# Joined norm and logarithm sums, and another opening of a three-block transformer kernel

## The chip, the cores and the metric

The kernel runs as one program on one core of a Trainium2 chip. A core has TensorE (PE in the rows: matmuls; PEld are its weight loads, which run beside them), VectorE (DVE), ScalarE (ACT), GpSimd (POOL) and SyncE (SP). Each engine works through its own instructions in a fixed order, and semaphores make one wait for another. Data comes from HBM by DMA: 16 DMA engines, fed by queues that SyncE, ScalarE or GpSimd start transfers on. The metric is the device time of one execution in microseconds (us), lower is better.

## What is computed

256 tokens of width 1024 go through a first block (four mixers, a feed-forward net, a gated per-layer input) and through two layers of a second block: dilated attention, a mixture of 16 experts, stick-breaking attention, a mixture of 16 experts. The parts that the change touches:

```python
def rmsnorm(x, g):
    x32 = x.astype(jnp.float32)
    y = x32 * lax.rsqrt(jnp.mean(x32 * x32, axis=-1, keepdims=True) + EPS)
    return (y * g.astype(jnp.float32)).astype(x.dtype)
...
def rope_tables(positions):
    inv = 1.0 / (ROPE_THETA ** (jnp.arange(0, QK_ROPE, 2, dtype=jnp.float32) / QK_ROPE))
    ang = positions.astype(jnp.float32)[..., None] * inv
    return jnp.cos(ang), jnp.sin(ang)
...
def layer_norm(x, g, b):
    xf = x.astype(jnp.float32)
    mu = xf.mean(-1, keepdims=True)
    var = jnp.square(xf - mu).mean(-1, keepdims=True)
    return ((xf - mu) * lax.rsqrt(var + LN_EPS) * g + b).astype(x.dtype)
...
def mixer_stick_breaking(x, w_in, w_out):
...
    z = jnp.clip(jnp.einsum('bhnqd,bhnkd->bhnqk', qb, kb).astype(jnp.float32), -SB_CLIP, SB_CLIP)
    sp = jnp.where(strict, jnp.log1p(jnp.exp(z)), 0.0)
    r_in = jnp.einsum('bhnqj,js->bhnqs', sp, suffix)
    att = jnp.where(strict, jnp.exp(z - r_in), 0.0)
```

`r_in` is a sum over the later keys of a row, here a matmul with a triangle of ones. There are 16 heads of width 64.

## The kernel before

Activations lie feature by feature: `x` is 128 partitions x 8 blocks x 256 tokens. Weights come in pieces of 128x2048, as two tiles of 128x1024 (512 KB each), from a list that `sequence` and `later_pieces` write out. For accuracy a weight piece is split (`wsplit`): ScalarE copies it to `whi` in the format F32R, VectorE subtracts to get `wlo`. Activations are split alike, into `x.hi` and `x.lo`. A projection (`proj`, by `mm3`) is then three F32R products for each weight block: whi with x.hi, whi with x.lo, wlo with x.hi. An f32 matmul, used where operands aren't split, shows as two records in the trace.

`piece` keeps one piece ahead: it starts the load and split of the next before the present is used. Loads go out on SyncE's queue in the order of the program and wait for a free `raw` buffer; a `raw` buffer is freed by the subtraction on VectorE, and a `whi`/`wlo` buffer by TensorE's last product with it.

The order on each engine is that of a scheduler that works from the program's order; `behind(...)` holds an instruction back behind another.

- Opening (`first`): SyncE loads `vecs` (gains and small vectors), the first weight tile of `w_a`, x in four parts of 256 KB between the next weight tiles (`part`, L725), constants and the positions in four small transfers (`rope_angles`, L617). GpSimd loads `rb`, the router's bias. While these land, 22 matmuls on ones run (`warm`, L258). `split_gain` makes gain times x, high on ScalarE and low on VectorE (tiles `gate`). `rstd` squares x on ScalarE, adds the squares on VectorE, sums over partitions by f32 matmuls with `ones` (`sc<-half,ones` or `acc<-half,ones`), takes the root on ScalarE and the reciprocal on VectorE. With `halve` it adds the two blocks of each tile first, so two matmuls instead of four. `rope_angles` makes the angles for cosine, then for sine, each with nine or more small VectorE operations.
- Later norms: in `first_tail` (`late`, the feed-forward stage and the one behind it) and in `dilated`, `rstd` is called without `halve`: four matmuls each.
- Second attention (`stick`): queries and keys of the first four heads are projected together (`begin`, `proj_beside`, two 128-blocks at a time, because the normed x arrives block by block), then per group of four heads ("quad"): `scores` of two heads, the value projection, `scores` of the other two, and beside the next group's projections `sums` and `outputs`. `scores` makes the logits `sbz` and their logarithm terms `sbl` (128x384: two row blocks of one head, the first with 128 keys, the second with 256) by absolute value, exponential and logarithm on ScalarE and mask on VectorE; `sums` multiplies `sbl` with the triangle (`k["suffix"]`, 384 columns) and with `ones` (128 columns) in f32.
- Norm over tokens (`token_norm`), at the end of each expert stage: x lies token by token (128 tokens x 1024, two halves `t`); VectorE adds the last experts' sum with a running total (L1820), ScalarE squares. Then for each half: mean, mean square, root, reciprocal, and x times 1/sigma minus mean/sigma, the first 512 columns on ScalarE and the others on VectorE. In the last layer (`along`) gain and offset follow as two passes of VectorE each (L239 `x<-x,s`), and each piece of 512 columns goes to `out`.

## Time and profile before

| what | us |
| --- | --- |
| median of 3 runs | 1289.57 (1289.53 to 1291.12) |
| the profiled execution | 1292.46 |
| its span | 1290.7 |
| TensorE busy in it | 1258.6 |
| VectorE, ScalarE busy | 731.3, 610.2 |
| moved by DMA | 268.28 MB |

The span runs from the first to the last instruction of the profiled execution, which itself is 2.9 us above the median. Busy times of engines overlap. TensorE's own time is counted from modelled ends, so a busy TensorE isn't always at its peak; its granted clock (PEclk) is given as a share of 2.4 GHz, and 0.50 is 1.2 GHz. In time the stages are: the first block's mixers 0 to 306 us (the opening to 36), the feed-forward net 306 to 517, the per-layer input 517 to 541, the first attention 541 to 838, its experts 838 to 984, a norm to 994, the second attention to 1122, routing to 1130, its experts to 1274, the last norm to the end.

### The profile page before, as it was taken

To read this page: it belongs to the slowest core of one execution; us is meant where nothing else is said; L and a number is where in the kernel's file an instruction comes from. 1 tells how busy PE (TensorE), PEld (TensorE's weight loads), DVE (VectorE), ACT (ScalarE), POOL (GpSimd) and SP (SyncE) were. 2 spreads that over 40 slices of the span, in tenths; PEclk is the share of its full clock that TensorE was granted. 3 is DMA by queue.
4 is the path that set the end of the run, shared out by engine and by line. 5 is a ranking of instruction groups with operands and counts; after the bars stand their busy time and mean duration, and the time that the engine had idled before them with its cause. 6 is when DMAs were issued, how large, how long until landed. Compare 5 with 4: busy or idle time off the path is not lost.

```text
span 1290.7 us, 22672 instructions
## 1 busy us (share of the span) xinstructions
PE 1258.6 (98%) x9159; PEld 1043.3 (81%) x9159; DVE 731.3 (57%) x1416; ACT 610.2 (47%) x951; POOL 24.8 (2%) x48
## 2 busy tenths in 40 slices
PE   9999999999999999999999999999998999999995
PEld 7987899999999999999999999855334999754332
DVE  7877667558665545876464646263215677454214
ACT  6674666446544544755454545232115666242112
POOL 0000000000000000000000000002000000002000
PEclk9999999999999999999999999999999999999998
DMA  7452346657486555566464645599999444557893
GB/s 263 147 183 71 109 137 204 187 178 241 142 300 229 178 186 176 185 190 187 141 194 134 194 134 170 166 318 332 358 395 370 131 131 131 191 196 272 331 397 132
DMA packets 91105, 268.28 MB, mean 208 GB/s; under 512 B 26528, under 2 KB 26672, under 8 KB 90736
## 3 DMA queue, kind: packets, MB, share of 16 engines
q1 hardware_dynamic: 86576, 252.80, 58.5%
q0 software_dynamic: 4416, 13.94, 3.2%
q8 instruction: 74, 1.21, 0.4%
q14 instruction: 39, 0.32, 0.1%
HBM read 267.68 MB, written 6.89 MB: 213 GB/s over the span
## 4 chain that ended last, share of the span: by engine, by line
PE 86%; DVE 5%; DMA 4%; ACT 3%; issue 1%; SPq 0%; ACTq 0%; DVEq 0%
PE ps L250 54%; PE acc L250 14%; PE y L250 6%; PE sc L250 4%; PE o L250 2%; PE sd L250 1%; PE o L258 1%; ACT whi L236 1%; DVE wlo L239 1%; PE sc L1265 1%; DMA raw<-e_d 1%; PE tr L250 1%; DMA s<-rows 1%; DMA wlo<-e_gu 1%; DMA raw<-e_gu 1%
## 5 line engine op out<-in xcount | busy, mean ns | idle before, releaser
L250 PE MATMUL ps<-s,whi 128*128 128x256 f32 x2656 | 495.0, 286 | 5.3 <-DVE s L239 2.5
L239 DVE TENSOR_TENSOR wlo<-raw,whi 128x1024 fp32r<-128x1024 f32 x276 | 333.8, 1218 | 258.5 <-ACT whi L236 258.0
L236 ACT ACTIVATE whi<-raw 128x1024 fp32r<-128x1024 f32 x276 | 287.1, 1054 | 307.1 <-PE ps L250 222.9
L250 PEld LDWEIGHTS ps<-s,whi 128*128 128x128 f32 x2656 | 414.9, 190 | 12.3 <-DVE s L239 4.0
L250 PE MATMUL ps<-s,wlo 128*128 128x256 f32 x1328 | 378.2, 285 | 1.3 <-DVE wlo L239 1.3
L250 PEld LDWEIGHTS ps<-s,wlo 128*128 128x128 f32 x1328 | 251.0, 189 | 4.6 <-DVE wlo L239 2.6
L250 PE MATMUL acc<-hid,whi 128*128 128x256 f32 x512 | 93.0, 281 | 0.0
L250 PE MATMUL ps<-whi,s 128*128 128x256 f32 x512 | 92.3, 282 | 0.0
L250 PE MATMUL ps<-raw,xg 128*64 128x512 f32 x344 | 86.2, 597 | 0.0
L250 PEld LDWEIGHTS ps<-whi,s 128*128 128x128 f32 x512 | 78.2, 188 | 1.5
L250 PEld LDWEIGHTS acc<-hid,whi 128*128 128x128 f32 x512 | 79.3, 189 | 0.0
L250 PE MATMUL acc<-hid,wlo 128*128 128x256 f32 x256 | 72.3, 283 | 0.0
L250 PE MATMUL ps<-wlo,s 128*128 128x256 f32 x256 | 71.7, 280 | 0.0
L250 PEld LDWEIGHTS ps<-raw,xg 128*64 128x64 f32 x344 | 25.7, 136 | 43.9 <-issue 40.5
L236 ACT ACTIVATE eh<-ps 128x256 f32<-128x256 f32 x16 | 6.2, 385 | 114.9 <-PE ps L250 114.9
L247 DVE SCALAR_TENSOR_TENSOR eh<-ps,gslot,eh 128x256 f32<-128x256 f32 x16 | 7.7, 484 | 85.2 <-ACT eh L236 85.2
L236 ACT ACTIVATE s<-y 128x512 fp32r<-128x512 f32 x36 | 21.0, 597 | 69.2 <-PE y L250 69.2
L239 DVE TENSOR_TENSOR s<-y,s 128x512 fp32r<-128x512 f32 x36 | 24.3, 686 | 50.6 <-ACT s L236 50.4
L250 PEld LDWEIGHTS ps<-wlo,s 128*128 128x128 f32 x256 | 48.1, 188 | 0.0
L250 PE MATMUL acc<-s,whi 128*128 128x256 f32 x256 | 47.7, 286 | 0.3 <-ACT dprobT L236 0.3
L250 PEld LDWEIGHTS acc<-hid,wlo 128*128 128x128 f32 x256 | 47.9, 187 | 0.0
L250 PE MATMUL y<-raw,hs 128*64 128x512 f32 x180 | 46.7, 600 | 0.0
(407 smaller groups left out, 1748.9 us busy)
## 6 DMA issues: line engine op xcount, KB each, us to landing
raw<-e_gu SPq DMA_DIRECT2D x81, 512.0 KB, 7.9
raw<-w_dil SPq DMA_DIRECT2D x72, 512.0 KB, 4.6
raw<-w_ff SPq DMA_DIRECT2D x64, 512.0 KB, 4.7
raw<-e_d SPq DMA_DIRECT2D x43, 512.0 KB, 10.1
raw<-w_g SPq DMA_DIRECT2D x32, 512.0 KB, 4.0
whi<-e_gu SPq DMA_DIRECT2D x31, 512.0 KB, 8.4
raw<-w_a SPq DMA_DIRECT2D x28, 512.0 KB, 4.8
raw<-w_sb SPq DMA_DIRECT2D x24, 512.0 KB, 7.8
```

Source lines behind the costliest of these rows:

```text
L236: return self.nc.scalar.activation(out, in_, func, **k)
L239: return self.nc.vector.tensor_tensor(out, a, b, op=op)
L247: return self.nc.vector.scalar_tensor_tensor(out, a, s, b, op0=op0, op1=op1, **k)
L250: self.last_mm = self.nc.tensor.matmul(out, l, r, start=first, stop=last, skip_group_check=True).ins,
L258: self.nc.tensor.matmul(p, self.ones_b, r, start=True, stop=True, skip_group_check=True)
L1265: nc.tensor.transpose(pt[:, c * 128:(c + 1) * 128], e[:, order[c]], self.k["ident"])
```

## The change

1. Opening. ScalarE starts x's four transfers ahead of its table load. The first weight tile comes as two transfers of 128x512 and is copied and subtracted in halves, with `split_gain` of two blocks behind each half's copy. The norm sum `rstd` is asked for right behind the first split. GpSimd starts the four position transfers (`rope_load`). Both angles are made at once in 128x2x64, by three-operand operations, and placed behind the last `split_gain`.
2. Norm sums. With `halve`, `rstd` now adds the last square into the total before it adds the halves, so one matmul remains of two; the three later norms are called with `halve` too.
3. Second attention. `sbl` is split into `sblh` and `sbll` (F32R), triangle and ones are copied to F32R, and each product becomes two. `begin` takes all products with `x.hi` first, then those with `x.lo`.
4. `token_norm`. The statistics of both halves are made two wide; in the last layer x plus minus-mean times gain is made while the root is taken, then times 1/sigma plus offset in one pass.
5. The last expert's `down` weights are asked for one step earlier (`down_weights`), `later_pieces` is called there, and `nhalf` is 3 in the second attention; no transfer on SyncE changes its place by this.

```diff
...
             raw = self.raw()
-            self.nc.sync.dma_start(raw[:, :k], src[:, c:c + k])
+            cuts = [slice(0, 512), slice(512, 1024)] if beside and not c else [slice(0, k)]
+            for u in cuts:
+                self.nc.sync.dma_start(raw[:, u], src[:, c + u.start:c + u.stop])
             then = beside and beside(c // 256)
             hi = self.W.tile([128, 1024], F32R, name="whi", bufs=self.nparts)
             lo = self.W.tile([128, 1024], F32R, name="wlo", bufs=self.nparts)
-            self.act(hi[:, :k], raw[:, :k], AF.Copy)
-            self.tt(lo[:, :k], raw[:, :k], hi[:, :k], OP.subtract)
+            for i, u in enumerate(cuts):
+                self.act(hi[:, u], raw[:, u], AF.Copy)
+                if then:
+                    then(i, len(cuts))
+                self.tt(lo[:, u], raw[:, u], hi[:, u], OP.subtract)
             his.append(hi)
             los.append(lo)
-            if then:
-                then()
...
-    def proj_beside(self, ws, kt, x, evacs, step):
+    def proj_beside(self, ws, kt, x, evacs, step, second=False):
 
 
         out = [self.ps() for _ in ws]
-        for k0 in range(0, kt, step):
+        for part in (0, 1) if second else ():
+            for k0 in range(0, kt, step):
+                for w, p in zip(ws, out):
+                    for b in range(2):
+                        for k in range(k0, min(k0 + step, kt)):
+                            for i, xp in ((0, x.lo),) if part else ((0, x.hi), (1, x.hi)):
+                                self.mm(p[:, b * S:(b + 1) * S], self.cut(w[i], k * S + b * 128, 128), xp[:, k],
+                                        not part and i == 0 and k == 0 and b == 0, part == 1 and k == kt - 1)
...
         if halve:
-            for t in both:
-                self.tt(t[:, 0], t[:, 0], t[:, 1], OP.add)
+            if len(both) > 1:
+                self.tt(tot, tot, both.pop(), OP.add)
+            self.tt(tot[:, 0], tot[:, 0], tot[:, 1], OP.add)
...
-    def rope_angles(self):
+    def rope_load(self):
         nc, A = self.nc, self.A
         tmp = self.row()
         pi = tmp[:, 192:].bitcast(I32)
         src = self.ap["pos"]
         for c in range(4):
-            nc.sync.dma_start(pi[32 * c:32 * c + 32], bass.AP(tensor=src.tensor, offset=src.offset + 64 * c,
-                                                              ap=[[0, 32], [1, 64]]))
-        ang, kk, t = (tmp[:, 64 * i:64 * i + 64] for i in range(3))
+            nc.gpsimd.dma_start(pi[32 * c:32 * c + 32], bass.AP(tensor=src.tensor, offset=src.offset + 64 * c,
+                                                                ap=[[0, 32], [1, 64]]))
...
-        for i, (q, sh) in enumerate(((0.25, math.pi / 2), (0.0, 0.0))):
-            r = self.trig[:, i]
-            self.ts(kk, ang, 1.0 / (2 * math.pi), OP.mult, q, OP.add)
-            self.ts(kk, kk, 12582912.0, OP.add, 12582912.0, OP.subtract)
-            for c, src in ((-TWO_PI_1, ang), (-TWO_PI_2, r), (-TWO_PI_3, r)):
-                self.ts(t, kk, c, OP.mult)
-                self.tt(r, t, src, OP.add)
-            self.ts(r, r, sh, OP.add, 3.1415925, OP.min)
-            self.ts(r, r, -3.1415925, OP.max)
-            if i:
-                self.ts(r, r, self.v("rope", 1), OP.mult)
+
+        kk = self.A.tile([128, 2, 64], F32, name="kk")
+        r, both = self.trig, ang[:, None, :].to_broadcast([128, 2, 64])
+        for i, q in enumerate((0.25, 0.0)):
+            self.ts(kk[:, i], ang, 1.0 / (2 * math.pi), OP.mult, q, OP.add)
+        self.ts(kk, kk, 12582912.0, OP.add, 12582912.0, OP.subtract)
+        for c, src in ((-TWO_PI_1, both), (-TWO_PI_2, r), (-TWO_PI_3, r)):
+            self.stt(r, kk, c, src, OP.mult, OP.add)
+        for i, sh in enumerate((math.pi / 2, 0.0)):
+            self.ts(r[:, i], r[:, i], sh, OP.add, 3.1415925, OP.min)
+        self.ts(r, r, -3.1415925, OP.max)
+        self.ts(r[:, 1], r[:, 1], self.v("rope", 1), OP.mult)
...
-        self.table("sqrt_and_others")
         self.sequence()
         x = self.x2()
+        for b in (0, 2, 4, 6):
+            self.tc.keep_in_program_order(nc.scalar.dma_start(x[:, b:b + 2], ap["xT"][:, b:b + 2]))
+        self.table("sqrt_and_others")
...
-            for b in (j, j + 2):
-                nc.sync.dma_start(x[:, b:b + 2], ap["xT"][:, b:b + 2])
-            return lambda: self.split_gain(h, x, "g_mix", range(j, j + 4))
+            return lambda i, n: self.split_gain(h, x, "g_mix", range(j + 4 * i // n, j + 4 * (i + 1) // n))
...
-                w = self.piece(beside=None if i else part)
+                if i == 0:
+                    self.make(1, part)
+                    r = self.rstd(x, 8, 1e-6, D, True)
+                w = self.piece()
                 if i == 0:
                     nc.sync.dma_start(self.cst, ap["consts"])
-                    self.rope_angles()
+                    angles = self.rope_load()
                 if i == 0:
                     self.proj_beside([w], 8, h, [lambda j, p: evac(0, p)], 4)
+                    with self.behind(self.last):
+                        self.rope_angles(angles)
...
-                rs.append(self.rstd(x, 8, 1e-6, D))
+                rs.append(self.rstd(x, 8, 1e-6, D, True))
...
+        if self.dense:
+            self.later_pieces()
         at = self.new_split(8)
         tiles = {}
+        suffix, ones = (A.tile([128, 128], F32R, name=n) for n in ("suffix_r", "ones_r"))
+        nc.vector.tensor_copy(suffix, self.k["suffix"])
+        nc.vector.tensor_copy(ones, self.ones)
...
-                             [ev("q", 0, 0.125), ev("k", 0, 1.0)], 2)
+                             [ev("q", 0, 0.125), ev("k", 0, 1.0)], 2, True)
...
-            ls = [A.tile([128, 384], F32, name="sbl", bufs=6) for _ in ps]
+            parts = [[A.tile([128, 384], F32R, name=n, bufs=4) for n in ("sblh", "sbll")] for _ in ps]
+            ls = [A.tile([128, 384], F32, name="sbl", bufs=2) for _ in ps]
...
+                self.act(hi, l, AF.Copy)
+                self.tt(lo, l, hi, OP.subtract)
+            tiles["z", quad, hp] = zs, parts
 
         def sums(quad, hp):
 
-            for z, l in zip(*tiles["z", quad, hp]):
+            for z, parts in zip(*tiles["z", quad, hp]):
                 pr = self.ps("sc")
-                self.mm(pr[:, :384], self.k["suffix"], l, True, False)
-                self.mm(pr[:, 128:256], self.ones, l[:, 256:384], False, True)
+                for i, l in enumerate(parts):
+                    self.mm(pr[:, :384], suffix, l, i == 0, False)
+                    self.mm(pr[:, 128:256], ones, l[:, 256:384], False, i == 1)
                 self.tt(z, z, pr[:, :384], OP.subtract)
...
+        self.tt(nm, sums[:, :, 0], sums[:, :, 1], OP.add)
+        self.ts(nm, nm, -1.0 / D, OP.mult)
+
+        def centre(t):
+            for c in cols:
+                self.stt(xr[:, t, c], xr[:, t, c], nm[:, t:t + 1], along[0][:, c], OP.add, OP.mult)
+        if along:
+            centre(0)
+        self.tt(u, nm, nm, OP.mult)
+        self.tt(rs, sqs[:, :, 0], sqs[:, :, 1], OP.add)
+        self.stt(rs, rs, 1.0 / D, u, OP.mult, OP.subtract)
+        self.act(rs, rs, AF.Sqrt, bias=self.eps[1e-5])
+        if along:
+            centre(1)
+        nc.vector.reciprocal(rs, rs)
+        if not along:
+            self.tt(nmr, nm, rs, OP.mult)
...
+                if along:
+                    self.stt(xr[:, t, c], xr[:, t, c], rs[:, o], along[1][:, c], OP.mult, OP.add)
+                    nc.sync.dma_start(self.out[t * 128:t * 128 + 128, c], xr[:, t, c])
+                elif n:
                     self.ts(xr[:, t, c], xr[:, t, c], rs[:, o], OP.mult, nmr[:, o], OP.add)
                 else:
                     self.act(xr[:, t, c], xr[:, t, c], AF.Identity, scale=rs[:, o], bias=nmr[:, o])
-                if along:
-                    self.tt(xr[:, t, c], xr[:, t, c], along[0][:, c], OP.mult)
-                    self.tt(xr[:, t, c], xr[:, t, c], along[1][:, c], OP.add)
-                    nc.sync.dma_start(self.out[t * 128:t * 128 + 128, c], xr[:, t, c])
```

ScalarE at the start of the program before (`whi<-raw` is the weights' high copy, `gate` the high part of x, `half` the squares for the norm, `x_74` is x):

```order
L480 ACT_TABLE_LOAD
L236 ACTIVATE whi<-raw 128x1024
L236 ACTIVATE gate<-x_74,vecs 128x256 x2
L236 ACTIVATE half<-x_74 128x512
L236 ACTIVATE gate<-x_74,vecs 128x256 x2
L236 ACTIVATE half<-x_74 128x512
L236 ACTIVATE whi<-raw 128x1024
L236 ACTIVATE gate<-x_74,vecs 128x256 x2
```

and after (`x_73` is x):

```order
L738 DMA x_73<-xT 128x512 x4
L495 ACT_TABLE_LOAD
L236 ACTIVATE whi<-raw 128x512
L236 ACTIVATE gate<-x_73,vecs 128x256 x2
L236 ACTIVATE whi<-raw 128x512
L236 ACTIVATE gate<-x_73,vecs 128x256 x2
L236 ACTIVATE whi<-raw 128x1024
L236 ACTIVATE gate<-x_73,vecs 128x256 x2
L236 ACTIVATE half<-x_73 128x512
L236 ACTIVATE gate<-x_73,vecs 128x256 x2
L236 ACTIVATE half<-x_73 128x512 x3
```

The four transfers of x stand in front of the table load, the first high copy is cut in two with two blocks of x behind each half, and three squares stand ahead of the next weight piece.

TensorE at the end of the first two projections of the second attention before (`s_10704` is the normed and split x; where it stands first the product belongs to queries or keys, where the weights stand first to values; `sc<-dq,dk`, the first scores, follow 13 value products):

```order
L250 MATMUL ps<-s_10704,whi 128x256 x2
L250 MATMUL ps<-s_10704,wlo 128x256
L250 MATMUL ps<-whi,s_10704 128x256 x2
L250 MATMUL ps<-wlo,s_10704 128x256
L250 MATMUL ps<-whi,s_10704 128x256 x2
```

and after (`s_10685` is the normed and split x):

```order
L250 MATMUL ps<-s_10685,whi 128x256
L250 MATMUL ps<-s_10685,wlo 128x256
L250 MATMUL ps<-s_10685,whi 128x256 x32
L250 MATMUL ps<-whi,s_10685 128x256 x2
L250 MATMUL ps<-wlo,s_10685 128x256
L250 MATMUL ps<-whi,s_10685 128x256 x2
L250 MATMUL ps<-wlo,s_10685 128x256
L250 MATMUL sc<-dq,dk 128x256 x2
```

The products with the low half, spread among the others before, now stand together in one run of 32 at the end; and 6 products of the value projection, instead of 13, come ahead of the first scores.

VectorE in the last norm before (`tn_m` mean, `tn_r` 1/sigma, `tn_u` its square, `tn_b` the shift, `s` gain and offset):

```order
L247 SCALAR_TENSOR_TENSOR tn_r<-tn_r,tn_u 128x1
L239 TENSOR_TENSOR tn_r<-tn_q 128x1
L247 SCALAR_TENSOR_TENSOR tn_r<-tn_r,tn_u 128x1
L1832 RECIPROCAL tn_r<-tn_r 128x1
L239 TENSOR_TENSOR tn_b<-tn_m,tn_r 128x1
L244 TENSOR_SCALAR x_12315<-x_12315,tn_r,tn_b 128x512
L1832 RECIPROCAL tn_r<-tn_r 128x1
L239 TENSOR_TENSOR x_12315<-x_12315,s_12907 128x512 x4
L239 TENSOR_TENSOR tn_b<-tn_m,tn_r 128x1
L244 TENSOR_SCALAR x_12315<-x_12315,tn_r,tn_b 128x512
L239 TENSOR_TENSOR x_12315<-x_12315,s_12907 128x512 x4
```

and after:

```order
L239 TENSOR_TENSOR tn_m<-tn_s 128x2
L243 TENSOR_SCALAR tn_m<-tn_m 128x2
L247 SCALAR_TENSOR_TENSOR x_12396<-x_12396,tn_m,s_12988 128x512 x2
L239 TENSOR_TENSOR tn_u<-tn_m 128x2
L239 TENSOR_TENSOR tn_r<-tn_q 128x2
L247 SCALAR_TENSOR_TENSOR x_12396<-x_12396,tn_m,s_12988 128x512
L247 SCALAR_TENSOR_TENSOR tn_r<-tn_r,tn_u 128x2
L247 SCALAR_TENSOR_TENSOR x_12396<-x_12396,tn_m,s_12988 128x512
L1877 RECIPROCAL tn_r<-tn_r 128x2
L247 SCALAR_TENSOR_TENSOR x_12396<-x_12396,tn_r,s_12988 128x512 x4
```

Statistics are two wide, the centring passes stand between them, and behind the reciprocal four pieces of one pass remain of eight.

## Rows read from the trace of the kernel before

**Rows 1.** The page, part 4: the chain of waits, share of the span by engine.

```profile
PE 86%; DVE 5%; DMA 4%; ACT 3%; issue 1%; SPq 0%; ACTq 0%; DVEq 0%
```

**Rows 2.** Windows: length, busy us (x) of PE, PEld, DVE, ACT, POOL; PEclk, DMA, GB/s.

```profile
306.00:517.00 211.00, 210.50 (x1728) 207.61 (x1727) 122.21 (x139) 103.05 (x124) 1.25 (x2) 1.00 0.64 208
...
1018.00:1122.00 104.00, 104.00 (x820) 93.25 (x817) 68.53 (x142) 60.78 (x102) 0.00 (x0) 1.00 0.45 143
...
1130.00:1274.00 144.00, 141.96 (x686) 65.30 (x685) 47.51 (x143) 34.40 (x67) 8.27 (x10) 1.00 0.79 289
...
998.00:1001.00 3.00, 3.00 (x15) 3.00 (x16) 2.91 (x8) 2.18 (x3) 0.00 (x0) 0.50 0.04 18
```

**Rows 3.** Chain of waits, the opening (start, length, what).

```profile
1.66 5.85 DMA x<-xT
...
35.00 1.15 DVE wlo L239
```

**Rows 4.** Groups by shape, VectorE, 19 to 36 us (busy, mean ns | idle before).

```profile
L243 DVE TENSOR_SCALAR row<-row 128x64 f32<-128x64 f32 x6 | 1.1, 181 | 0.0
```

**Rows 5.** DMA, 0 to 15 us: GB/s in 40 slices; packets, MB, share by queue.

```profile
GB/s 0 0 0 0 34 213 276 317 339 175 165 71 48 70 18 115 317 388 421 415 410 404 393 393 399 415 459 399 426 404 415 415 397 411 391 398 411 346 415 393
...
q0 software_dynamic: 32, 0.01, 7.5%
```

**Rows 6.** Groups by shape, TensorE, whole span (two records for one f32 matmul).

```profile
L250 PE MATMUL sc<-half,ones 128*128 128x256 f32 x28 | 7.5, 388 | 0.0
...
L250 PE MATMUL acc<-half,ones 128*128 128x256 f32 x16 | 3.9, 379 | 0.0
```

**Rows 7.** Chain of waits at one norm and at the second attention.

```profile
529.31 1.73 PE acc L250 x8
...
997.84 14.35 PE ps L250 x105
...
1018.34 5.95 PE ps L250 x48
1024.29 1.73 PE sc L250 x8
```

**Rows 8.** Timeline, TensorE, the sums of one head (start, length, what).

```profile
1024.13 0.81 PE L250 MATMUL sc<-sbl,consts 128*128 128x384 f32 x2
1024.78 0.38 PE L250 MATMUL sc<-sbl,ones 128*128 128x128 f32 x2
```

**Rows 9.** Timeline, a pair of heads: its last mask, its first sum.

```profile
1039.62 0.49 DVE L239 TENSOR_TENSOR sbl<-sbl,consts 128x128 f32<-128x128 f32 x2
...
1048.44 0.81 PE L250 MATMUL sc<-sbl,consts 128*128 128x384 f32 x2
```

**Rows 10.** Groups, VectorE, 1027 to 1100 us, second attention.

```profile
L239 DVE TENSOR_TENSOR wlo<-raw,whi 128x1024 fp32r<-128x1024 f32 x19 | 23.2, 1223 | 10.2 <-ACT whi L236 10.0
...
L247 DVE SCALAR_TENSOR_TENSOR sbl<-sbz,sbl 128x384 f32<-128x384 f32 x12 | 6.7, 555 | 7.9 <-ACT sbl L236 7.9
```

**Rows 11.** Windows, 24 us of that attention, about one group of four heads.

```profile
1026.00:1050.00 24.00, 24.00 (x192) 21.73 (x191) 17.86 (x38) 16.26 (x28) 0.00 (x0) 1.00 0.42 132
```

**Rows 12.** Timeline, start of the second attention ([idle before <- releaser]).

```profile
996.08 0.39 PE L250 MATMUL ps<-s,whi 128*128 128x256 f32 x1 [1.19 <-DVE s L239]
...
997.84 0.55 PE L250 MATMUL ps<-s,whi 128*128 128x256 f32 x1 [1.14 <-DVE s L239]
...
1001.69 0.42 DVE L239 TENSOR_TENSOR s<-x,s 128x256 fp32r<-128x256 f32 x1
```

**Rows 13.** Chain of waits, the last norm.

```profile
1277.12 0.19 DVE tn_m L239 x2
...
1279.87 1.89 DVE x L239 x3
...
1282.45 2.50 DVE x L239 x4
```

**Rows 14.** Groups by shape, VectorE, three-operand work on 128x512, whole span.

```profile
L247 DVE SCALAR_TENSOR_TENSOR x<-x,s 128x512 f32<-128x512 f32 x8 | 5.1, 686 | 0.9 <-DMA s<-rows 0.9
```

More of the change, by code (lines that the diff above doesn't have):

```diff
@@ L347, in piece, with make @@
     def piece(self, n=1, beside=None):
-        while len(self.made) < n + 1 and self.pieces:
+        self.make(n + 1, beside)
+        now, self.made = self.made[:n], self.made[n:]
+        return now if n > 1 else now[0]
+    def make(self, n, beside=None):
+        while len(self.made) < n and self.pieces:
             src, width = self.pieces.pop(0)
@@ L352, in piece @@
             beside = None
-        now, self.made = self.made[:n], self.made[n:]
-        return now if n > 1 else now[0]
     @staticmethod
@@ L1739, in hidden, with down_weights, down @@
             return hs
-        def down(i, hs):
+        def down_weights(i):
+            return wsp[1] if i == 8 else self.beside([ap["e_d"][layer, 2 * i + s] for s in range(2)], 2048)
+        def down(i, hs, wd=None):
             yparts.append(yparts.pop(0))
             y = yparts[0]
-            wd = wsp[1] if i == 8 else self.beside([ap["e_d"][layer, 2 * i + s] for s in range(2)], 2048)
+            wd = wd or down_weights(i)
             for n in range(2):
```

37 lines of the change are left out of this document (18 added, 19 removed).

## The prediction

> **What bounds the kernel now.** I read the chain of waits by engine first: 86% of the span is TensorE at work or feeding itself [rows 1]. So most stages end when TensorE has worked off its queue, and a matmul taken out is worth its own time there, while work moved among the other engines is worth nothing unless TensorE stands for it. The windows say where that holds: the feed-forward stage keeps TensorE busy 210.50 of 211 us and the second attention 104.00 of 104, with the DMA engines at 0.45 in the latter, while the second expert stage runs its DMA at 0.79 [rows 2]. Three short stretches are bound otherwise, and the change edits each of them. In the opening TensorE waits first for x, which lands 1.66 + 5.85 = 7.5 us after the start, then for VectorE's backlog up to 35.00 + 1.15 = 36.15 us [rows 3]. At the start of the second attention it waits for the low halves of the normed input (1.19 and 1.14 us, [rows 12]) and then runs at a granted clock of 0.50, the 1.2 GHz level, for 3 us [rows 2]. Behind the last matmul, VectorE does the last norm alone: from 1277.12 to 1284.95 us [rows 13].
>
> **Opening.** Two ends meet. For the front: x now goes out on ScalarE's queue instead of between the weight pieces, and the first weights are split in halves. x shares the engines with the weights either way; over 400 GB/s flow from about 6.4 us on, but before that lies a lull down to 18 GB/s [rows 5], so I take no earlier x and 0.4 us for the halves. For the back: VectorE is the bound to 36 us, and 11 of 23 small angle operations go. Six of them are recorded at 181 ns [rows 4]; their records overlap, so I count 0.15 us each, 1.65 us. Against that stand two wider operations, one more 128x512 addition of the sum of squares and the cut subtraction, together about 0.8 us. The reciprocal no longer stands behind the angles, which now come behind the first split. ScalarE squares x before it converts the next weight piece, which holds TensorE up by up to 0.8 us, but the stage ends with VectorE. Net **-0.8 us**, between -1.8 (the removed work whole) and +0.8 (ScalarE's delay whole).
>
> The Trainium skill, "DMA: Bandwidth & Descriptors", section "Issuing engines are not separate DMA queues", says that transfers started by different engines run on the same 16 DMA engines, and that starting them from several saves only issue time. The lull and the plateau of this trace agree with it. By it alone the front gives nothing and the sum below would be 0.4 us smaller.
>
> Positions move to GpSimd's queue behind the router's bias. Off SyncE that frees issue time nobody waits for; what it may cost is rival 1.
>
> **Norm sums.** Three norms (in the feed-forward, behind it, and in the first attention) fold four squares into one before the ones-matmul: 4 f32 matmuls become 1. A group of four takes 1.73 us, 0.43 each [rows 7]. The counts before are 8 and 14 (two records each, [rows 6]); the order shows 2 and 10 after. Of the 10 removed one is in the opening, where TensorE isn't the bound; 9 x 0.43 = **-3.9 us**. VectorE adds a 128x512 and loses none, 0.6 us per norm, in stages where it is busy 122 of 211 us [rows 2]. If a projection's result then waits for the norm for lack of a free PSUM bank, 0.3 us per norm is lost: bounds -3.0 to -4.0.
>
> **Suffix sums of the second attention.** Now each head has one f32 product of 384 columns and one of 128: a head is half of a pair's 1.73 [rows 7], 0.87 us, of which 1024.13 to 1024.78 is the first product, 0.65 [rows 8], and 0.22 the second. After, each is two F32R products, of the high and the low part. F32R at 256 columns goes at 5.95 / 48 = 0.124 us [rows 7]; for 384 I scale it to 0.18. At 128 columns F32R isn't in these rows: from 0.062 (scaled) to 0.22 (what f32 takes at that shape). I take 0.17, halfway from the row of the same format (0.124) to that of the same shape (0.22). 2 x (0.18 + 0.17) = 0.70; 16 heads x 0.17 = **-2.7 us**, between -1.1 and -6.2.
> The parts cost ScalarE a copy and VectorE a subtraction of 128x384, some 0.55 us a head [rows 10], with a new wait: VectorE stands for ScalarE's copy, and behind it in its queue lie the weights' low halves. The cover is large: a pair's last mask starts at 1039.62 and its sum at 1048.44 [rows 9], and two heads' copies and subtractions take 2.2 of those 8 us, 3.5 with two waits of 0.66 (worked out in rival 3). The f32 buffers shrink from six to two, but two heads are in work at a time. So I cost it at nothing; rival 3 is what it costs if the cover is gone.
>
> **Start of the second attention.** The first two projections (96 products) take all products with the high half first (64), then those with the low half (32). Before, four products stand ahead of 997.84 with two waits, 1.19 and 1.14 us [rows 12]; the chain's 105 from there to 1012.19 [rows 7] are the other 92 and 13 of the value projection, so the 96 end at 1012.19 - 13 x 0.124 = 1010.6. After, high products run while the low halves are made; the last of these is done at 1001.69 + 0.42 = 1002.1 [rows 12], and if only the 32 low products are left then, they end at 1002.1 + 32 x 0.124 = 1006.1. With part of the half clock [rows 2] left I take 1007: 3.6 us won. Some comes back, since the high weights are now needed in both passes and their buffers come free later, so the value weights are converted later and the first scores wait for them, by my estimate 0.6 to 1.2 us (a weight piece's high copy and subtraction take turns on both engines; the subtraction takes 1.22 us, [rows 10]). Net **-2.8 us**, between -0.5 (half clock stays and the scores wait 2 us) and -4.0.
>
> **Last norm.** Before, eight two-operand passes stand behind the statistics: 1.89 us for three, 2.50 for four [rows 13]. After, two passes (centre and gain, then scale and offset) of four pieces each, three-operand; these are recorded at 686 ns [rows 14], paced like the others at 2.50 / 4 = 0.62. From 1277.12: mean 0.25, four centred pieces 2.50, beside them two-wide statistics 0.5, reciprocal 0.2, four pieces 2.50: 1283.0 instead of 1284.95, and the wait of about 0.4 us for the root is covered by centring. Outputs now leave 0.62 us apart, about what one 256 KB transfer takes at 400 GB/s, so 0.1 us is lost at the end. **-1.9 us**, between -1.0 and -2.3. The same statistics in the first layer: **-0.2** (0 to -0.5). The earlier asking for the last expert's weights and the smaller buffer count move no transfer: 0.
>
> **Sum.** -0.8 - 3.9 - 2.7 - 2.8 - 1.9 - 0.2 = -12.3 us. The profiled execution took 1292.46 us (span 1290.7), 2.9 over the median of 1289.57; the same steps from the median give **1277.3 us**. All good ends give 1270.3, all bad ones 1284.8.
>
> **Rivals.**
> 1. The four position loads stall the opening. The software queue's 32 packets (8 KB) hold 7.5% of 16 engines for 15 us [rows 5], 1.1 us of all engines, while the rate falls to 18 GB/s. Four more such loads, in front of x and the first weights: up to 4.5 us. For it: the lull is there and nothing else explains it; against: it may be paid once. 1277.3 + 0.8 + 4.5 = **1282.6**. 12%.
> 2. What the second attention gains is lost behind it, because the second expert stage is set by its weights (DMA 0.79, [rows 2]). The 2.7 + 2.8 go: **1282.8**. Against: the weights come as buffers fall free, which TensorE's pace sets, at 0.45 before that stage. 14%.
> 3. Slower: VectorE becomes the bound of the second attention. Per group of four heads (24.3 us, from 1024.13 to 1048.44, [rows 8, 9]) VectorE is busy 17.9 us of 24 [rows 11], idle 6.2. Added are 4 x 0.55 = 2.2 us and 4 waits for the copy, each as long as today's for ScalarE, 7.9 / 12 = 0.66 [rows 10], 2.6 us. If none of the idle time gives way, a group takes 24.3 + 4.8 = 29.1 us; four groups and the lost 2.7 give 1277.3 + 19.2 + 2.7 = **1299.2**. It turns slower than before from 24.3 + 9.6 / 4 = 26.7 us a group. Against: over the 73 us of these rows, three groups, 10.2 of some 18.6 idle us are waits for weights [rows 10] whose buffers TensorE frees, and these shrink. 5%.
> 4. The reordering does not do what it says: the half clock and the buffers eat the whole 2.8, and F32R at 128 columns costs what f32 does (another 1.6): 1277.3 + 4.4 = **1281.7**. 15%; the forecast itself 54%.
>
> **How the numbers follow.** About 0.2%, 2.6 us, is what a measurement of this kernel can tell, so faster means below 1287.0. The forecast and rivals 1, 2 and 4 lie there, unless two of them meet: faster 0.88. Two meeting with the bad ends of other terms: same 0.07; rival 3 past its point: slower 0.05. The range takes in rivals 1, 2 and 4 and half of the good ends: 1272.5 to 1284.5.
>
> **What would show it.** Opening: VectorE's backlog ends near 35.4 instead of 36.15; rival 1 shows as x landing after 9 us. Norms: one ones-matmul where four stood. Sums: the pair's 1.73 us becomes about 1.4. Second attention: no wait for low halves, the first two projections end about 3 us earlier in the stage. End: VectorE's part, from the mean to its last pass, takes 5.9 us instead of 7.8. The prediction is wrong if the expert stages grow by what the stages ahead of them shrink, or if groups of four heads take longer than 24.3 us.

## The result, and the profile after

| | before | after |
| --- | --- | --- |
| median of 4 runs each on one chip, us | 1290.09 (1289.53 to 1291.12) | 1278.74 (1278.42 to 1279.50) |
| ratio after / before | | 0.9912 (95% interval 0.9895 to 0.9929) |
| profiled execution, us | 1292.46 | 1278.75 |
| its span, us | 1290.7 | 1276.8 |

The change takes 11.35 us off (9.2 to 13.5 by the interval); 12.3 were forecast. The two traces differ by 13.9 us, because the profiled execution of before lay above its median and that of after did not. So a stage is judged below by several traces, not by this pair alone. Executions of one kernel differ with the granted clock: of seven executions of before on one chip, three took 1288.96 to 1289.35 us at a mean granted clock of 0.993, and four took 1291.8 to 1292.48 at 0.990 or 0.991.

The page of after, its busy times (part 1) and its chain of waits by engine (part 4):

```profile
PE 1245.2 (98%) x9139; PEld 1037.0 (81%) x9139; DVE 737.0 (58%) x1413; ACT 613.1 (48%) x964; POOL 26.7 (2%) x52
...
PE 83%; DMA 8%; DVE 4%; ACT 3%; issue 1%; SPq 0%; DVEq 0%; ACTq 0%; POOL 0%
```

TensorE is busy for 13.4 us less, 1245.2 instead of 1258.6, and that is nearly the whole difference of the spans; some 3 us of it aren't work taken out but two stretches in which before ran at the lower clock (both below). VectorE and ScalarE are busy for longer. In the chain DMA has 8% instead of 4% [rows 1]. Little of that is the opening, whose DMA link grows from 5.85 to 9.64 us; most are six links of weights from 931.33 to 987.18 us, in the first expert stage and the norm behind it, where before's chain runs over the engines. That stage isn't longer for it: from the first attention's routing to the last expert sums it takes 155.6 us instead of 156.1.

Where the time went, between instructions that both traces name. The third column is the profiled execution of after less that of before (what is not listed makes up the other 0.8 us), the fourth what the experiments leave of it:

| stretch | forecast | the two traces | by the runs below |
| --- | --- | --- | --- |
| opening, to the first matmul on the angles (`sd<-trig,half`) | -0.8 | +0.7 | +0.7, in other traces up to +1.6 |
| 54 to 82 us, where the clock differs | 0 | -1.5 | 0 |
| feed-forward stage, first norm | -1.3 | -1.2 | -1.25 |
| per-layer input to first attention, second and third norm | -2.6 | -1.4 | -1.4 |
| last expert sums to the first scores of the second attention | -3.0 | -3.4 | -3.4 (of it -1.5 by the clock) |
| first scores to the routing | -2.7 | -3.9 | -3.9 (sums -4.65, +0.8 given back) |
| second expert stage | 0 | -1.0 | 0, 148.8 to 150.4 us in all kernels |
| last norm | -1.9 | -1.4 | -1.45 |
| sum | -12.3 | -13.1 | -10.7 |

The sum of the last column and the median agree within 0.7 us. That the sum came out near the forecast is in part luck, since misses of both signs cancel: opening and norm sums brought 2.7 us less than forecast and the last norm 0.4, the second attention 1.6 more, of which 1.5 is a clock that no run ties to the change.

The second line isn't the change. TensorE's granted clock in 54 to 82 us, before and after (windows; columns as in [rows 2]):

```profile
54.00:82.00 28.00, 26.62 (x203) 25.59 (x203) 23.92 (x51) 17.76 (x27) 0.26 (x2) 0.94 0.52 166
```

```profile
54.00:82.00 28.00, 26.62 (x213) 25.10 (x211) 24.76 (x54) 18.79 (x29) 0.26 (x2) 1.00 0.52 169
```

At 0.94 fewer instructions fit into the same 28 us. From the first `sd<-trig,half` to the first `ps<-whi,a4p`, 224 matmul records on, before took 30.2 or 30.3 us in its two traces. Of the kernels below whose TensorE order is after's up to there, five took 30.2 or 30.3 as well (`pos_sync`, `norm3_old`, `begin_old`, `sums_f32`, `lo_twice`), while two (`norm2_old`, `tail_old`) took 28.7, as after itself did in both its traces. So this 1.5 us isn't to be put down to the change.

### The profile page after: what moved, and what is told of

Same layout as the page of the kernel before. It is cut to its first block, busy times and chain, and to the rows that moved or that the text cites. A ratio compares the mean times of both kernels' runs of the same rounds, so it can differ in the third digit from the quotient of the medians.

```text
span 1276.8 us, 22646 instructions
## 1 busy us (share of the span) xinstructions
PE 1245.2 (98%) x9139; PEld 1037.0 (81%) x9139; DVE 737.0 (58%) x1413; ACT 613.1 (48%) x964; POOL 26.7 (2%) x52
## 4 chain that ended last, share of the span: by engine, by line
PE 83%; DMA 8%; DVE 4%; ACT 3%; issue 1%; SPq 0%; DVEq 0%; ACTq 0%; POOL 0%
PE ps L250 54%; PE acc L250 13%; PE y L250 5%; PE sc L250 4%; PE o L250 2%; DMA wlo<-e_gu 2%; DMA raw<-w_sb 1%; PE sd L250 1%; DMA raw<-e_d 1%; PE sc L1289 1%; ACT whi L236 1%; DVE wlo L239 1%; DMA s<-rows 1%; PE tr L250 1%; DMA whi<-e_d 1%
## 5 line engine op out<-in xcount | busy, mean ns | idle before, releaser
L239 DVE TENSOR_TENSOR wlo<-raw,whi 128x1024 fp32r<-128x1024 f32 (+1 forms) x277 | 333.4, 1213 | 243.9 <-ACT whi L236 243.3
L236 ACT ACTIVATE whi<-raw 128x1024 fp32r<-128x1024 f32 (+1 forms) x277 | 286.5, 1049 | 296.9 <-PE ps L250 213.4
L239 DVE TENSOR_TENSOR s<-y,s 128x512 fp32r<-128x512 f32 x36 | 24.2, 685 | 50.6 <-ACT s L236 50.5
```

The lines of the kernel that those rows point to most:

```text
L236: return self.nc.scalar.activation(out, in_, func, **k)
L239: return self.nc.vector.tensor_tensor(out, a, b, op=op)
```

## Experiment: is it the opening, and which part of it?

The forecast was that VectorE's backlog ends near 35.4 us. It ends at 35.69 + 1.15 = 36.84, later than the 36.15 of before [rows 3]. The chain of waits of after in the opening (start us, length, what):

```profile
2.13 9.64 DMA raw<-w_a
...
11.79 1.07 ACT whi L236
...
35.69 1.15 DVE wlo L239
```

The first DMA link is no longer x but the second tile of the first weights, 9.64 us on its way, to 11.77 us. Three kernels take this apart; `before_again` gives before's own spread, with nothing changed.

> The kernel before, unchanged, for a second trace. Theory: the profiled execution of before ran about 2.4 us above its median because of two stretches that belong to that run and not to the kernel, a granted clock of 0.94 in 54 to 82 us (58 products in 8.65 us instead of 7.14) and about 1 us in the second expert stage; the second trace then has a span near 1288.3 us, and the matmuls on a4p that end at 81.1 us end near 79.6. Rival: these stretches are the kernel's, the span is again near 1290.7 and the clock again 0.94 there; then the change gained 13.9 us in the trace and something outside of the span took 2.5 back.

Measured: 1291.04 us, span 1289.3, with the opening at 51.1 us as in the first trace of before. The theory missed on the clock, which was 0.94 in 54 to 82 us again. The span is 1.4 us shorter, 1.1 of it in the two expert stages, where the theory had 1 us in the second.

`old_opening` has the parts of the diff in `wsplit`, `split_gain`, the angles and `first` undone, and nothing else.

> The kernel after with the opening of before (loads, weight halves, order of squares, angles one after the other). Theory: the new opening loses 0.7 us by the time VectorE's backlog ends (36.84 against 36.15 us), so this kernel is 0.7 us faster than the kernel after, about 1278.0, and the product run behind the backlog starts near 36.2 us. Rival (the forecast): the new opening is worth 0.8 us, so this kernel takes about 1279.5.

`pos_sync` moves only the positions back:

```diff
-            nc.gpsimd.dma_start(pi[32 * c:32 * c + 32], bass.AP(tensor=src.tensor, offset=src.offset + 64 * c,
+            nc.sync.dma_start(pi[32 * c:32 * c + 32], bass.AP(tensor=src.tensor, offset=src.offset + 64 * c,
```

> The kernel after with the four position transfers back on SyncE's queue, x still by ScalarE's. If the position transfers on GpSimd's queue hold up the first weights (rival 1 of the prediction), the second weight half lands 1 to 4 us before 9.89 us and the backlog of VectorE ends 1 us or more before 36.84: about 1277.5. If it is x on a queue of its own, with all transfers in flight at once, that makes the weights late, nothing moves before 12 us and the time is that of the kernel after, 1278.7, within 0.5.

`x_sync` moves only x back between the weight tiles on SyncE's queue:

```diff
-        for b in (0, 2, 4, 6):
-            self.tc.keep_in_program_order(nc.scalar.dma_start(x[:, b:b + 2], ap["xT"][:, b:b + 2]))
...
+            for b in (j, j + 2):
+                nc.sync.dma_start(x[:, b:b + 2], ap["xT"][:, b:b + 2])
```

> The kernel after with x back on SyncE's queue between the weight tiles, positions still by GpSimd's. If x on its own queue makes the weights late, the second half lands at about 6 instead of 9.87 us and the second tile near 10 instead of 11.77, the first projection ends about 2 us before 20.1 and VectorE's backlog near 35.5 instead of 36.84: 1277.4. If GpSimd's transfers are the cause, the first half is still late (after 6.2 us) and the backlog ends near 36.8: 1278.7.

Measured, on one chip with before at 1291.8 us (1288.96 to 1292.48):

| kernel | us | ratio to before | backlog ends | `sd<-trig,half` starts |
| --- | --- | --- | --- | --- |
| before | 1291.8 | | 36.15 | 51.1 |
| after | (another chip) | 0.9912 | 36.84 | 51.8 |
| old_opening | 1279.62 | 0.9916 (0.9898 to 0.9934) | 36.19 | 51.1 |
| pos_sync | 1279.17 | 0.9910 (0.9892 to 0.9927) | 36.85 | 51.8 |
| x_sync | 1278.05 | 0.9902 (0.9881 to 0.9923) | 35.16 | 50.1 |

The medians lie within 1.6 us and tell the three apart badly; the traces do it better. The opening of after varies, though: in the nine traces on this page that have x on ScalarE's queue, `sd<-trig,half` starts at 51.8 to 52.7 us, in the middle at 52.3, so +0.7 is the least that it loses against before, which has 51.1 in both its traces. `pos_sync` changes nothing (36.85 against 36.84), so the positions on GpSimd's queue cost nothing that shows beside this spread, far from the 4.5 us of rival 1: it falls. `x_sync` is where the time is. ScalarE's first weight copies in after and in `x_sync` (timeline: start, length, what, in brackets the idle time before it and what ended it):

```profile
6.24 0.63 ACT L236 ACTIVATE whi<-raw 128x512 fp32r<-128x512 f32 x1 [2.32 <-DMA raw<-w_a]
...
9.89 0.63 ACT L236 ACTIVATE whi<-raw 128x512 fp32r<-128x512 f32 x1 [2.22 <-DMA raw<-w_a]
...
11.79 1.06 ACT L236 ACTIVATE whi<-raw 128x1024 fp32r<-128x1024 f32 x1 [0.47 <-DMA raw<-w_a]
```

```profile
5.97 0.63 ACT L236 ACTIVATE whi<-raw 128x512 fp32r<-128x512 f32 x1 [3.94 <-DMA raw<-w_a]
...
7.48 0.63 ACT L236 ACTIVATE whi<-raw 128x512 fp32r<-128x512 f32 x1 [0.87 <-DMA raw<-w_a]
```

With x on a queue of its own, ScalarE gets the second half of the first weights at 9.89 us, 2.4 us later than the 7.48 of `x_sync`, and waits 2.22 us for it. x itself doesn't come late. Its first part with ScalarE's queue (chain of `pos_sync`), and with SyncE's, with the end of the backlog there (chain of `x_sync`):

```profile
0.75 3.94 DMA x<-xT
```

```profile
2.13 6.02 DMA x<-xT
...
34.01 1.15 DVE wlo L239
```

It lands at 4.69 instead of 8.15 us. All 1 MB of x is then in flight beside the weights, though the first two blocks of it are all that the first half needs; on one queue it comes in the order of need. The DMA engines' rate in after (GB/s in 40 slices of 0 to 15 us, as in [rows 5]):

```profile
GB/s 0 0 0 0 34 100 158 251 295 330 354 382 291 205 164 147 160 198 298 344 354 411 384 438 388 403 445 437 396 404 423 396 426 419 430 397 416 405 427 412
```

The rate climbs more slowly, 100 and 158 in the sixth and seventh slice where before had 213 and 276, but the dip behind the first transfers is filled in the main (147 instead of 18). By 6 us, 16 slices, 1.02 MB have come instead of 0.69. So the second queue does bring data earlier, only not the data that the first projection waits for.

What is left of the new opening in `x_sync` is worth -1.0 us against before (50.1 against 51.1), by the end of the backlog too (35.16 against 36.15). That is near the forecast's -0.8 and its 35.4. How much of it the weight halves bring and how much the fewer angle operations, no run separates. The queue for x takes 1.7 us away here.

`after_again` and `x_sync_again` are the same two kernels, on one chip, five executions each, to see whether the version with x on SyncE beats the change.

> The kernel after, unchanged, beside the next one on the same chip. If the stretch from 52 to 80 us at a granted clock of 0.94 or 1.00 comes and goes, its length is 28.7 or 30.2 us whichever the kernel; the opening ends at 51.8 us or a little more as before; total about 1279.

> The kernel after with x back on SyncE's queue, beside the kernel after on the same chip. Theory: its opening ends 1.7 us earlier (50.1 against 51.8), nothing later gives it back, so its median is 1.7 us below that of the kernel after. Rival: a later stage that the weights' transfers bound takes it back, and the two agree within 0.5 us.

Measured beside before at 1290.64 us: after 1279.97 (1279.25 to 1281.63), ratio 0.9922 (0.9908 to 0.9935); with x on SyncE 1277.55 (1276.51 to 1279.69), ratio 0.9900 (0.9886 to 0.9913). The medians differ by 2.4 us and the openings in the traces by 2.5 (52.4 against 49.9); the intervals still touch. In the two traces of `x_sync` the stretch of 54 to 82 us was at the lower clock (30.2 us) and in the two of after at the full one (28.7), so the profiled spans are closer than the medians, 1276.8 each in the first pair. With that said, x on SyncE's queue is the fastest version here, by the opening in both its traces and by the median in both comparisons, the first of them across two chips.

## Experiment: what are the norm sums worth?

All three stand as one matmul (two records) where four stood. After, from the second norm to behind the third (chain of waits; start, length, what):

```profile
526.91 0.43 PE acc L250 x2
527.34 15.75 PE ps L250 x132
543.09 1.19 DVE s L247 x3
544.27 1.18 DVE wlo L239
545.46 0.61 DVE half L239
...
546.20 11.76 PE ps L250 x96
557.96 0.43 PE sc L250 x2
558.39 21.48 PE ps L250 x179
```

Each group takes 0.43 instead of 1.73 us [rows 7], as forecast. The feed-forward stage is indeed 1.25 us shorter, in every kernel that has its norm halved. The other two should give 2.6 together and give 1.4: from the start of the second group to the end of the third, before takes 32.9 us (529.31 to 560.46 + 1.73 = 562.19) and after 31.5 (526.91 to 558.39). In between stands a wait that before doesn't have. After, and before (timeline of TensorE, columns as above):

```profile
546.20 0.47 PE L250 MATMUL ps<-s,whi 128*128 128x256 f32 x2 [1.59 <-DVE half L239]
```

```profile
550.21 0.38 PE L250 MATMUL ps<-s,whi 128*128 128x256 f32 x1 [0.34 <-DVE s L247]
```

1.59 us of waiting instead of 0.34 is the missing 1.2. I first took it that the second norm alone was eaten by a stretch bound by VectorE, and undid one norm at a time.

`norm3_old`:

```diff
-                    r = self.rstd(x, 8, 1e-6, D, True)
+                    r = self.rstd(x, 8, 1e-6, D)
```

> The kernel after, with the third of the later norms (first attention) back at four ones-matmuls. In the trace of after TensorE waits 1.6 us for VectorE's adding of squares (544 to 546 us), which wasn't there before. Theory: that wait eats the 1.3 us of this norm, so from the per-layer products (517.7 before, 515.3 after) to the first attention's value products (588.0, 584.2) this kernel takes 68.9 us as after does, and the time is that of after within 0.3 us. Rival (the forecast): the norm gained its 1.3 us and the stretch takes 70.2 us.

`norm2_old` (`one[0]` is true for the first of these norms and set false behind it):

```diff
-                rs.append(self.rstd(x, 8, 1e-6, D, True))
+                rs.append(self.rstd(x, 8, 1e-6, D, one[0]))
```

> The kernel after with the second of the later norms (behind the feed-forward) back at four ones-matmuls. With the third norm undone, the stretch between the per-layer products and the first attention's value products had grown from 68.9 to 70.1 us, of 70.3 before, so the third norm has its 1.2 us and the second cannot have more than 0.2. Theory: TensorE's saved 1.3 us ends in the 1.59 us wait behind VectorE's drain of a projection (at 546 us), a stretch that VectorE bounds; then this kernel keeps 68.9 within 0.2 us and its wait there shrinks to 0.3. Rival: both norms gained and something else lost; then the stretch takes 70.2.

Measured: 1281.39 and 1280.39 us, one execution each. From the end of the feed-forward stage to the first product behind the third norm's stage, before takes 70.3 us, after 68.9, `norm3_old` 70.2, `norm2_old` 70.1. So each of the two norms is worth 1.2 to 1.3 when the other is there, and my theory that the second was worth nothing falls. Both kernels still wait 1.6 us for `half` at the same product, so the wait belongs to neither of them alone: a kernel with one of them undone is no faster than before in this stretch, because it pays the wait and has one gain to set against it.

What the wait is, the instruction order with its waits shows. The waiting product is the first of a projection: with it 96 products stand in the chain up to the third norm's sum; before, 13 of these ran ahead of its stall, which left 83. TensorE's instructions stand in the same order there in both kernels, but the projection's first product waits for other things. Before, then after:

```
L250 MATMUL ps_6306<-s16_6248,whi_6184 128x256 [waits Activation_49]
```

```
L250 MATMUL ps_6296<-s16_6238,whi_6174 128x256 [waits DVE_49,Activation_49]
```

It now waits for VectorE too, and what VectorE finishes just ahead of 546.20 is `half<-ps,rstd` (L239), the pass that takes the projection just ahead out of PSUM, the memory that matmuls write to. The built programs say why. The waiting projection has PSUM bank 0 in both kernels; the projection just ahead of it has bank 2 in before and bank 0 in after, and there the next one has to wait until VectorE has taken its result out. With only the second or only the third norm as in before, it stays bank 0, as the waits of `norm2_old` and `norm3_old` show. With only the first norm as in before, the program has bank 2 and before's waits again. So it is the first norm's shorter sum that moves the bank, and the 1.2 us would be a price of that norm, nearly all of the 1.25 us that it brings. That kernel was read and not run, so this price is argued, while the wait and its 1.2 us are measured.

## Experiment: the suffix sums

After, the sums of a pair of heads (chain of waits, then the timeline of TensorE):

```profile
1011.64 5.95 PE ps L250 x48
1017.59 1.10 PE sc L250 x8
```

```profile
1017.43 0.34 PE L250 MATMUL sc<-sblh,suffix_r 128*128 128x384 f32 x1
1017.60 0.23 PE L250 MATMUL sc<-sblh,ones_r 128*128 128x128 f32 x1
1017.66 0.39 PE L250 MATMUL sc<-sbll,suffix_r 128*128 128x384 f32 x1
1017.90 0.22 PE L250 MATMUL sc<-sbll,ones_r 128*128 128x128 f32 x1
1017.96 0.39 PE L250 MATMUL sc<-sblh,suffix_r 128*128 128x384 f32 x1
```

From start to start, a product of 384 columns takes 0.17 to 0.24 us and one of 128 columns 0.06. A pair takes 1.10 us instead of 1.73 [rows 7], where 1.40 were forecast.

`sums_f32` has before's f32 products (`sblh`, `sbll` and the F32R copies of triangle and ones are gone), `lo_twice` makes each low part twice, which loads VectorE with as much again:

```diff
-                self.tt(lo, l, hi, OP.subtract)
+                for _ in range(2):
+                    self.tt(lo, l, hi, OP.subtract)
```

> The kernel after with the suffix sums back in f32 (no split of the logarithm terms). After, a pair of heads' sums takes 1.10 us in the chain where before had 1.73. Theory: the eight pairs are all that the sums gained, so from the first attention's router product (825.1) to the second's last (1113.1) this kernel takes 5.0 us more than the 288.0 of after. The forecast had 2.7 us. Rival: the added copies and subtractions cost TensorE waits, then it is less than 5.

> The kernel after with each low part of the logarithm terms subtracted twice: one more VectorE operation of 128x384, 0.55 us, for each of 16 heads. If the 8 us of cover between a pair's last mask and its sum hold, the second attention keeps its length within 0.3 us. If VectorE is near to being its bound (rival 3 of the prediction), each group of four heads grows by up to 2.2 us and the stage by up to 8.8.

Measured: 1283.71 and 1280.24 us, one execution each, before at 1290.97. From the first scores to the routing's last product, after takes 108.40 us, `sums_f32` 113.04, `lo_twice` 108.40. So the split sums are worth 4.65 us, 0.4 less than eight pairs at 0.63 (where that goes stays open), and twice the low part costs nothing: the cover that the forecast counted on holds with room to spare, and rival 3 falls. How VectorE pays for it (groups by shape, 1020 to 1093 us; busy, mean ns, idle before) in `sums_f32`, after and `lo_twice`:

```profile
L239 DVE TENSOR_TENSOR wlo<-raw,whi 128x1024 fp32r<-128x1024 f32 x19 | 23.2, 1223 | 9.9 <-ACT whi L236 9.7
```

```profile
L239 DVE TENSOR_TENSOR wlo<-raw,whi 128x1024 fp32r<-128x1024 f32 x19 | 23.2, 1222 | 3.3 <-ACT whi L236 2.9
...
L239 DVE TENSOR_TENSOR sbll<-sbl,sblh 128x384 fp32r<-128x384 f32 x13 | 7.2, 553 | 0.6 <-ACT sblh L236 0.6
```

```profile
L239 DVE TENSOR_TENSOR wlo<-raw,whi 128x1024 fp32r<-128x1024 f32 x19 | 23.2, 1221 | 0.0
L239 DVE TENSOR_TENSOR sbll<-sbl,sblh 128x384 fp32r<-128x384 f32 x28 | 15.0, 553 | 0.2
```

VectorE's idle time ahead of the weights' low halves shrinks from 9.9 to 3.3 to nothing as the low parts are added, and TensorE's pace stays. The wait for ScalarE's copy, which the forecast bounded by 0.66 us each, is 0.6 us over 13 of them.

## Experiment: the start of the second attention and the norms over tokens

`begin_old` takes the first two projections in before's order (`2, True` becomes `2` in the call); `tail_old` has before's `token_norm`, in both layers.

> The kernel after with the second attention's first two projections in the order of before (high, low and low-weight products together). Forecast: the new order is worth 2.8 us, so the stretch from the norm's statistics to the first scores grows by 2.8 us, with waits for the low halves of about 2.3 us and a stretch at half clock. Rival: the new order gains nothing beyond the two-wide statistics, and the stretch stays within 0.5 us, because weight buffers come free later.

> The kernel after with the norm over tokens of before in both layers. Theory: from the last mean (1264.7) to the end it takes 13.5 us as before instead of 12.1, and from the first layer's running totals (980.7) to the second attention's first scores (1004.74) 25.2 us instead of 24.04, since undoing the order of the first projections gave only 2.2 of the 3.35 us that this stretch gained. Forecast: 14.0 at the end (1.9 us) and 24.2 at the first (0.2 us). Rival for the first: the 1.2 us belong to the earlier asking for the last weights, then it stays at 24.0.

Measured: 1281.13 and 1280.93 us, one execution each. In the table the first column runs from the first read of the last expert sums' total (`tn_s`) to the first scores, the third from the last read of the last norm's totals to the end of the span:

| kernel | to the first scores | first scores to routing | last norm |
| --- | --- | --- | --- |
| before, twice | 27.4, 27.4 | 112.3, 112.2 | 13.6, 13.6 |
| after | 24.0 | 108.4 | 12.2 |
| begin_old | 26.3 | 107.5 | |
| tail_old | 23.6 | | 13.6 |

The order of the products brings 2.3 us up to the scores and gives 0.9 back behind them, 1.4 net. Before's order with everything else of the change is already 1.1 us faster than before, and the chains show how. Before, then `begin_old`:

```profile
997.84 14.35 PE ps L250 x105
```

```profile
995.37 12.84 PE ps L250 x105
1008.21 0.02 issue
1008.23 0.92 PE sc L250 x8
```

The same 105 products behind the same waits take 1.5 us less. Windows of 1 us in before (as in [rows 2]) and in `begin_old`:

```profile
999.00:1000.00 1.00, 1.00 (x7) 1.00 (x6) 0.91 (x3) 1.00 (x2) 0.00 (x0) 0.50 0.01 4
```

```profile
997.00:998.00 1.00, 1.00 (x11) 1.00 (x10) 0.92 (x3) 0.98 (x3) 0.00 (x0) 1.00 0.00 0
```

Before runs these products at a granted clock of 0.50 (1.2 GHz) for some 3 us, in both its traces; `begin_old`, in before's order, at 1.00. In the 3 us ahead (995 to 998 and 992 to 995 us) TensorE was busy 0.78 us in before and 1.01 us in `begin_old`, so it had stood still for most of the time in both. Why the clock falls in one and not in the other, no run here separates, and it stays open; the 1.5 us are therefore not shown to be the change's. In after TensorE is busy 2.69 us of the 4 up to 992, and the products run at 1.00:

```profile
992.45 12.29 PE ps L250 x100
1004.74 0.87 PE sc L250 x8
```

The two-wide statistics don't help at this place: with the old ones (`tail_old`) the scores come 0.4 us earlier in the stretch, where the forecast had -0.2. The shift `tn_b`, which ScalarE's half of the norm waits for, in after and in `tail_old` (timeline of VectorE):

```profile
987.16 0.15 DVE L239 TENSOR_TENSOR tn_b<-tn_m,tn_r 128x2 f32<-128x2 f32 x1
```

```profile
986.25 0.16 DVE L239 TENSOR_TENSOR tn_b<-tn_m,tn_r 128x1 f32<-128x1 f32 x1
```

The total's first read is at 980.70 and 980.80. With one shift for both halves it comes behind one more weight subtraction than the first half's shift had to wait for. So the stretch's -3.4 are -2.3 by the order, -1.5 by the clock and +0.4 by the statistics.

At the end of the program the new `token_norm`, two-wide statistics and single pass together, is worth the whole 1.45 us: 12.2 us with the new form, 13.6 with the old, as in before. The last norm of after (chain; the mean ends at 1264.91):

```profile
1264.74 0.17 DVE tn_m L239
...
1265.19 1.41 DVE x L247 x2
...
1268.06 0.17 DVE tn_r L1877
...
1268.96 2.03 DVE x L247 x3
```

From the mean to the last pass it takes 1270.99 - 1264.74 = 6.25 us, where before took 7.8 [rows 13] and 5.9 were forecast. A centring pass takes 0.70 us (1.41 for two) and not the 0.62 assumed.

## Why the prediction was right, point by point

- **What bounds the kernel** held in the main: TensorE is busy for 13.4 us less and the span fell with it, some 3 us of that by the clock. That the added work of VectorE costs nothing was tried in the second attention (`lo_twice`) and held there.
- **Opening** failed: +0.7 instead of -0.8. The step that failed is "I take no earlier x and 0.4 us for the halves": x's queue was taken as neutral because the engines are shared "either way", and the lull to 18 GB/s was read as agreeing with that. But the lull fills when a second queue is there, x's first part lands 3.5 us earlier, and the weights that are needed ahead of most of x land 2.4 us later. With x back on SyncE the rest of the term held (-1.0).
- **Rival 1** fell: the positions' queue is worth 0.0 us in one pair of traces. Its sign, x landing after 9 us, could not have told it apart: what came late by x's own queue was a weight half, not the first x.
- **Norm sums** had the right price for each matmul (0.43 us) and the right kind of trouble, a projection waiting for a PSUM bank, but not its place and size: "0.3 us per norm", for which the prediction shows no row, was a bound of 0.9 in all, and one wait of 1.2 us more came between the second and the third norm. Measured -2.65 instead of -3.9, outside the bounds of -3.0 to -4.0.
- **Suffix sums** were mis-sized in the term "I take 0.17, halfway": 128 columns in F32R go at 0.06 us, which is the bound scaled by columns from the 256-column row. Measured -4.65 instead of -2.7, inside the bounds.
- **Start of the second attention** came out at -3.4 to the scores, with 0.8 given back behind them: -2.6 against -3.0. The number is near by luck. The scheme (high products first, some of it given back) held in kind, but the order is worth 1.4 net where 2.8 were forecast; the two-wide statistics cost 0.4 instead of bringing 0.2; and 1.5 is the half clock, which is gone in `begin_old` too, without the new order. That the value weights are what gives the time back was not tested.
- **Last norm** -1.45 against -1.9: a wider pass than assumed, 0.08 us each.
- **Rival 2** fell: the second expert stage takes 148.8 to 150.4 us in all kernels, and what the attention gains reaches the end. **Rival 3** fell with `lo_twice`. **Rival 4** fell on F32R at 128 columns, which is cheaper, not dearer; of the reordering's 2.8 us half is there, so on that count it was half right.
- **The bounds**: all good ends add up to 18.8 us, so to 1270.8 and not 1270.3 us; the range doesn't hang on it.

## What to carry to other kernels

A queue of its own brings an early input sooner, and everything on it then competes with what is needed first; so in an opening like this one keep the transfers on one queue in the order of need, and check by the landing time of the first weights. Where an edit shortens TensorE's work, look at the first products behind it for a new wait: here a shorter group shifted the PSUM bank that a later projection gets, and half of the gain of two groups stood there. Cover for added work is best read from the idle time ahead of the engine's own loads, here 9.9 us that shrank to 3.3 with no effect on the pace, and not from its share of busy time.

## What the runs showed of the hardware that was not expected

- The 4 position loads of 8 KB on GpSimd's queue, beside x and the first weights, cost 0.0 us in the opening (36.84 with them, 36.85 without, one trace each; kernels with the same opening differ by up to 0.9).
- The granted clock fell to 0.50 for some 3 us in before behind a stand of TensorE and stayed at 1.00 in `begin_old` behind a like one, with the same instructions behind it; 1.5 us hang on it.
- A stretch of 54 to 82 us ran at a mean granted clock of 0.94 or of 1.00 with the same instructions on TensorE, 1.5 us apart, which is as much as a term of the sum.
- x on a second queue raised what the DMA engines moved in the first 6 us from 0.69 to 1.02 MB, and the opening still became longer.
